# T4 taken plainly in the second group, its quarter sums spread over the third, weighings in idle PSUM banks, and the last product in column halves

## The chip, the cores and the metric

One core of one Trainium2 chip. The metric is the device time of one execution in microseconds (us). Before the change it is 1509.28 us, the median of 3 runs (1508.52 to 1510.85).

## The reference

```python
def reference(x, w):          # x: 8 x 2048 x 2048, w: 2048 x 2048, both f32
    cs = np.cumsum(x, axis=1)
    diff = cs - np.concatenate([np.zeros(...), cs[:, :-1, :]], axis=1)
    return np.matmul(diff, w).astype(np.float32)
```

The difference of a running sum is x again, so the work is one product of 16384 x 2048 by 2048 x 2048.

## The kernel before

Rows of x come in tiles of 128. Four tiles of the start are multiplied directly while w arrives. Then groups of four tiles follow: g, g+1 and h, h+1 (h = g+2). Each pair is one block product in Winograd's form, with seven half-size products where eight would be needed: B11, T1, B12 and so on are f16 blocks and sums of blocks of w, S1 to S4 sums of blocks of x. From the second group on, three of the products of each pair (with B21, B22 and T4) are split in the same way once more, which makes 28 matmuls of 2 x 16 = 32. They need the quarter sums `in2`, `in3` and `in4`, which VectorE makes once. The group that TensorE works on from about 75 to 126 us, which has none of this inner splitting yet, is called the plain group here, and the next ones the second, third and so on.

A tile of x goes through these steps: a load; a *weighing* on ScalarE (a sum of absolute values, whose elementwise output is scrap); a scale from it; a *narrowing* to f16 on ScalarE; a transpose by DMA. A weighing is either whole (`weigh`, with an output slot `c` as scrap) or in four pieces (`weigh_in`, with a pair of PSUM banks as scrap):

```python
def keep(dst, ps, scale):     # copy out of PSUM, ScalarE
    for c, p in pieces_of(dst, ps):
        after("act", lambda: nc.scalar.activation(c, p, COPY, scale=scale))

def add(dst, ps, scale):      # add out of PSUM, VectorE
    for c, p in pieces_of(dst, ps):
        after("dve", lambda: nc.vector.scalar_tensor_tensor(c, p, scale, c, MUL, ADD))

def less_in(Q1, Q2, Q4, t11, t12, t21, t22):
    less(Q1, t12, t11)        # four subtractions each
    less(Q2, t22, Q1)
    less(Q4, t21, Q2)
def less_in3(Q1, Q2, Q4, t11, t12, t21, t22):
    less(t12, t22, t12)

def weigh(t, slot):
    xf = came.pop(t)
    m, _ = after("act", lambda: measure(xf, new_c(slot)))       # one ACTIVATE of 2048
    got[t] = m, None, xf
def weigh_in(t, ps):          # cut: four ACTIVATEs of 512 into ps[i % 2], then a reduce on VectorE
    ...

def group_plain(g, X, Y, Z, V, a, b, c, d):
    # ... cut
    product(Z, S1, T1, True)
    # ... cut
    fetch_x(h + 5)
    weigh(g + 5, c)           # the first weighing that the change touches (about 116 us)
    scale_of(g + 5)
    C22 = new_c(d)
    keep(C22, Z, vh)          # TensorE's wait near 118 is for these copies
    product(X, A22g, T4, False)
    C21 = new_c(b)
    keep(C21, X, vg)
    ready(g + 5)              # the narrowing
    turn(g + 5)               # the transpose
    put(C21, g + 1, 0)
    product(Y, A21h, T3, False)
    add(C22, Y, vh)
    put(C22, h + 1, 1)
    less_in(*in2)
    less_in3(*in2)
    product(Z, S4h, B22, False)
    # ... cut
    less_in(*in3)
    product(Y, A22h, T4, False)
    # ... cut

def group(g, X, Y, Z, V, a, b, c, d):
    # ... cut
    keep(C11g, X, ug)
    S3g = sums(g, S4g)
    if second:
        weigh(h + 1, c)       # the second one (about 132 us)
        ready(h + 1)
        less_in(*in4)
    turn(h + 1)
    fetch_x(h + 4)
    product(Y, A11h, B11, True)
    if second:
        weigh_in(g + 4, V)
    # ... cut
    inner_product(A2, in2, banks, C11g, C11h, *u, between_2)
    if second:
        less_in3(*in3)
        less_in3(*in4)
    # ... cut, then four(): A22 T4 in quarters, or in the last group:
    def four_last():
        # ... cut
        product_in(q, s2, Q2, False)
        add(C21g[:, NB:], q, vg)
        put(C21g, g + 1, 0)
        product_in(Y[0], a22, Q4, False)
        keep(C21h[:, :NB], Y[0], vh)
        product_in(q, s3, Q3, False)
        for n in range(2):
            at = ds(n * NB, NB)
            add(C21h[:, at], q, vh)
            nc.scalar.dma_start(out2[ds((h + 1) * P, P), at], C21h[:, at])
```

The order of the source is not quite the order of the matmuls: the compiler moves some of TensorE's matmuls ahead of one that would wait.

Of the kernel before, what the change touches and what calls it, by code (L numbers as in the profile page):

```python
# [33 lines left out]
def kernel(  # L34
# [6 lines left out]
    nc = tc.nc  # L41
    P = 128
# [7 lines left out]
    NB = 512  # L50
# [14 lines left out]
    PLAIN = 4  # L65
# [78 lines left out]
    with tc.tile_pool(name="ring", bufs=7) as ring, tc.tile_pool(  # L144
# [97 lines left out]
        def put(c, rows, columns, queue=nc.gpsimd):  # L242
            return queue.dma_start(out2[rows, columns], c)
# [221 lines left out]
    def product(ps, a, b, first):  # L465
        for k in range(KH):
            for n in range(NH // NB):
                nc.tensor.matmul(  # L468
                    ps[n],
                    a[k],  # L470
                    b[k][:, n, :],
                    start=(first and k == 0),
                    stop=(k == KH - 1),
                    skip_group_check=True,
                )

    def product_in(ps, a, b, first):
        for k in range(4):
            nc.tensor.matmul(  # L479
                ps, a[k], b[k], start=(first and k == 0), stop=(k == 3), skip_group_check=True  # L480
            )
# [13 lines left out]
    def keep(dst, ps, scale):  # L495
        for c, p in pieces_of(dst, ps):
            after("act", lambda: nc.scalar.activation(c, p, COPY, scale=scale))  # L497

    def add(dst, ps, scale):
        for c, p in pieces_of(dst, ps):  # L500
            after(
                "dve", lambda: nc.vector.scalar_tensor_tensor(c, p, scale, c, MUL, ADD)  # L502
            )
# [9 lines left out]
    def less(dst, p, q):  # L513
        for k in range(len(dst)):
            after("dve", lambda: nc.vector.tensor_tensor(dst[k], p[k], q[k], SUB))  # L515


    def less_in(Q1, Q2, Q4, t11, t12, t21, t22):
        less(Q1, t12, t11)
# [6 lines that stand above are left out]
    def new_c(slot):  # L526
        return cpool.tile([P, NH], f32, name=f"c{slot}")
# [5 lines left out]
    def fetch_x(t):  # L533
        if t < END:
            came[t], _ = after("sp", lambda: bring(t))

    def weigh(t, slot):
        if t < END:
            xf = came.pop(t)
            m, _ = after("act", lambda: measure(xf, new_c(slot)))  # L540
            got[t] = m, None, xf
# [94 lines left out]
    def sums(t0, S4=None):  # L636
        A11, A12 = parts(t0)
        A21, A22 = parts(t0 + 1)
        total(S1, A21, A22, ADD)
        total(S2, S1, A11, SUB)  # L640
        total(A21, A11, A21, SUB)
        if S4:
            total(S4, A12, S2, SUB)
        return A21


    def group_plain(g, X, Y, Z, V, a, b, c, d):
# [67 lines left out]
        ready(h + 4)  # L715
        turn(h + 4)
        fetch_x(h + 5)
        weigh(g + 5, c)
        scale_of(g + 5)
        C22 = new_c(d)  # L720
        keep(C22, Z, vh)
# [20 lines left out]

    def group(g, X, Y, Z, V, a, b, c, d):
        h = g + 2
        second = g == PLAIN + 4
        A11g, A12g = parts(g)
        A11h, A12h = parts(h)
        A21g, A22g = parts(g + 1)
# [7 lines left out]
        C11g = new_c(a)  # L756
        keep(C11g, X, ug)
        S3g = sums(g, S4g)
        if second:
            weigh(h + 1, c)  # L760
            ready(h + 1)
            less_in(*in4)
        turn(h + 1)
        fetch_x(h + 4)
        product(Y, A11h, B11, True)
# [20 lines left out]
        total(A21h, A11h, A21h, SUB)  # L786
        total(S2, S1, A11h, SUB)
        S3h = A21h
        product(X, S3g, T3, False)
        add(C22, X, vg)  # L790
        put(C22, g + 1, 1)
# [13 lines left out]
        inner_product(A2, in2, banks, C11g, C11h, *u, between_2)  # L805
        if second:
            less_in3(*in3)
            less_in3(*in4)
        total(S4h, A12h, S2, SUB)
        turn(h + 4)  # L810
        put(C11h, h, 0)
# [1 line left out]
        one, two, A3 = sums_in(S4g, S4h, S0, S3g)  # L813
        one()
        two()

        product(Y, S2, T2, False)
        C12h = new_c(d)
# [2 lines left out]
        C22 = new_c(a)  # L821
        keep(C22, Z, vh)
        add(C12h, Z, uh)
        weigh(g + 5, b)
        one, two, A4 = sums_in(A22g, A22h, S1, S2)

# [8 lines left out]
        def seven():  # L835
            product(Y, S3h, T3, False)
            add(C22, Y, vh)
            put(C22, h + 1, 1)


        def four():
# [30 lines left out]
        def four_last():  # L872
            a11, a12, a22, s1, s2, s3, s4 = A4
            Q1, Q2, Q4, t11, Q3, t21, t22 = in4
            C21g, C21h = new_c(b), new_c(c)
            product_in(q, a11, t11, True)
            keep(C21g[:, :NB], q, vg)
            product_in(X[0], a12, t21, False)
            add(C21g[:, :NB], X[0], vg)
            product_in(X[1], s4, t22, False)  # L880
            keep(C21g[:, NB:], X[1], vg)
            product_in(e, s1, Q1, True)
            add(C21g[:, NB:], e, vg)
            keep(C21h[:, NB:], Y[1], vh)
            add(C21h[:, NB:], e, vh)
            product_in(q, s2, Q2, False)
            add(C21g[:, NB:], q, vg)
            put(C21g, g + 1, 0)
            product_in(Y[0], a22, Q4, False)
            keep(C21h[:, :NB], Y[0], vh)  # L890
            product_in(q, s3, Q3, False)
            for n in range(2):
                at = ds(n * NB, NB)
                add(C21h[:, at], q, vh)
                nc.scalar.dma_start(out2[ds((h + 1) * P, P), at], C21h[:, at])

        inner_product(A3, in3, banks, C12g, C12h, *u, between_3)
        put(C12h, h, 1)
        one()
        two()  # L900
        seven()
        (four if g + 4 < END else four_last)()

    fetch_x(PLAIN + 4)
    banks = [bank(i) for i in range(8)]
# [36 lines left out]
```

## Time and profile before

| | before |
|---|---|
| median time | 1509.28 us |
| span of the profiled execution | 1507.3 us |
| TensorE busy | 99% |
| VectorE, ScalarE busy | 73%, 57% |
| matmul to matmul, 512 columns | 0.216 us |
| one steady group, 212 matmuls | 45.80 us |

A line of the timeline gives start, duration, engine, source line, operation, output and inputs, shape and count; in brackets the idle time of the engine just before and what ended it. TensorE's ends are modelled (0.38 us for a matmul of which one starts every 0.216 us), so the bracket is some 0.16 us smaller than the true loss. Below, "wait" with three digits is the time from start to start beyond 0.216 us, and a bracket is called a bracket. The lines that the argument rests on stand in the prediction.

### The profile page before, as it was taken

The page shows a single profiled execution, that of the slowest core. Times are in us where ns is not written, and L with a number is a line of the kernel's source. Part 1 is how long each engine was busy: PE and PEld are TensorE (multiplying, and loading weights), DVE is VectorE, ACT ScalarE, POOL GpSimd, SP SyncE. Part 2 cuts the span into 40 slices and gives each one's busy share as a digit, 9 for nine tenths or more (in the row PEclk, how much of TensorE's full clock was granted, in tenths as well). Part 3 has the DMA queues.
Part 4 walks back from the last instruction along what each step waited for, and adds up shares of the span by engine and source line. Part 5 has one row for each costly group of instructions (what it writes and reads, how often), then busy time and mean ns, then how long its engine had stood idle before and what let it go on. Part 6 is the DMA issues. An engine that isn't in the chain of part 4 may idle for free.

```text
span 1507.3 us, 19123 instructions
## 1 busy us (share of the span) xinstructions
PE 1490.6 (99%) x6911; PEld 673.8 (45%) x6911; DVE 1104.4 (73%) x2053; ACT 864.5 (57%) x1107; POOL 5.2 (0%) x12
## 2 busy tenths in 40 slices
PE   8999999999999999999999999999999999999998
PEld 3444444444444444444444444444444444444443
DVE  7997777776677676777676776766776767776767
ACT  5875655565655566555656555655555565556551
POOL 0100000000000000000000000000000000000000
PEclk9999999999999999999999999999999999999999
DMA  9988878878978987888789788878788888887772
GB/s 362 351 250 233 236 224 246 234 213 227 235 225 244 224 224 236 215 246 236 210 229 232 230 241 217 235 222 248 216 244 207 236 221 250 232 236 216 223 208 112
DMA packets 322479, 351.50 MB, mean 233 GB/s; under 512 B 266896, under 2 KB 266896, under 8 KB 306512
## 3 DMA queue, kind: packets, MB, share of 16 engines
q1 hardware_dynamic: 321536, 347.92, 81.1%
q0 software_dynamic: 560, 1.84, 0.3%
q8 instruction: 54, 0.88, 0.2%
q10 hardware_dynamic: 288, 0.52, 0.1%
q14 instruction: 41, 0.34, 0.1%
HBM read 150.99 MB, written 134.22 MB: 189 GB/s over the span
## 4 chain that ended last, share of the span: by engine, by line
PE 88%; DVE 1%; DMA 1%; issue 0%; ACT 0%; DVEq 0%; ACTq 0%; SPq 0%
PE b L468 52%; PE b L479 36%; DVE c L502 1%; DMA fin<-in_x_dram 0%; DMA xT<-fin 0%; DVE W L511 0%; ACT b L553 0%; DVE W L515 0%; ACT c L497 0%; DVEq L937 0%; DVE xT L511 0%; DVE s L112 0%; DVE m L111 0%; DVE u L586 0%; DVE m L561 0%
## 5 line engine op out<-in xcount | busy, mean ns | idle before, releaser
L502 DVE SCALAR_TENSOR_TENSOR c<-b,u,c 128x512 f32<-128x512 f32 (+1 forms) x883 | 675.0, 799 | 234.8 <-ACT c L497 112.8
L497 ACT ACTIVATE c<-b,u 128x512 f32<-128x512 f32 x496 | 314.5, 680 | 265.4 <-PE b L468 170.5
L468 PE MATMUL b<-W,xT 128*128 128x512 f16 x2048 | 462.1, 379 | 0.8 <-ACT c L497 0.8
L468 PE MATMUL b<-W,W 128*128 128x512 f16 x1764 | 411.7, 379 | 1.8 <-ACT c L497 1.5
L105 ACT ACTIVATE c<-fin 128x2048 f16<-128x2048 f32 x92 | 175.7, 1910 | 242.4 <-DMA out_dram<-c 220.5
L468 PEld LDWEIGHTS <-xT 128*128 128x128 f16 x2048 | 200.4, 98 | 242.6 <-issue 1.1
L468 PEld LDWEIGHTS <-W 128*128 128x128 f16 x2016 | 197.2, 98 | 240.2 <-issue 2.1
L116 ACT ACTIVATE fin<-fin,s 128x2048 f16<-128x2048 f32 x123 | 246.3, 2002 | 93.8 <-issue 50.8
L479 PEld LDWEIGHTS <-W 128*128 128x128 f16 x1560 | 152.1, 98 | 187.5 <-issue 2.5
L479 PE MATMUL b<-W,W 128*128 128x512 f16 x810 | 220.0, 379 | 1.0 <-DVE c L502 1.0
L479 PE MATMUL b<-W,xT 128*128 128x512 f16 x720 | 180.0, 379 | 0.0
L479 PE MATMUL b<-inner,W 128*128 128x512 f16 x660 | 176.2, 379 | 0.0
L479 PEld LDWEIGHTS <-xT 128*128 128x128 f16 x960 | 93.9, 98 | 113.3
L561 DVE TENSOR_REDUCE m<-m 128x1 f32<-128x4 f32 x29 | 4.6, 157 | 106.7 <-ACT b L553 106.7
L553 ACT ACTIVATE b<-fin 128x512 f32<-128x512 f32 x116 | 67.8, 585 | 14.5 <-DMA fin<-in_x_dram 14.5
L468 PE MATMUL b<-W 128*128 128x512 f16 x252 | 75.0, 379 | 0.0
L511 DVE TENSOR_TENSOR W<-W,xT 128x1024 f16<-128x1024 f16 x122 | 68.2, 559 | 3.2
L511 DVE TENSOR_TENSOR W<-xT,W 128x1024 f16<-128x1024 f16 x122 | 67.5, 553 | 0.0
L479 PE MATMUL b<-inner,xT 128*128 128x512 f16 x240 | 61.6, 379 | 0.0
L233 PE MATMUL b<-wb,xP 128*128 128x512 bf16 x240 | 55.4, 383 | 5.9 <-ACT wb L216 4.8
L511 DVE TENSOR_TENSOR W<-xT,xT 128x1024 f16<-128x1024 f16 (+1 forms) x92 | 54.8, 596 | 0.0
L111 DVE TENSOR_SCALAR m<-m 128x1 f32<-128x1 f32 x124 | 18.5, 149 | 34.6 <-ACT c L105 33.5
(54 smaller groups left out, 457.9 us busy)
## 6 DMA issues: line engine op xcount, KB each, us to landing
out_dram<-c SPq DMA_DIRECT2D x247, 512.0 KB, 3.1
fin<-in_x_dram SPq DMA_DIRECT2D x123, 1024.0 KB, 5.5
W<-in_w_dram SPq DMA_DIRECT2D x32, 512.0 KB, 9.6
W<-in_x_dram SPq DMA_DIRECT2D x16, 256.0 KB, 7.4
xT<-fin SPq DMA_TRANSPOSE x184, 5.2
out_dram<-o POOLq DMA_DIRECT2D x7, 256.0 KB, 3.9
out_dram<-o SPq DMA_DIRECT2D x7, 256.0 KB, 4.1
xP<-in_x_dram SPq DMA_DIRECT2D x1, 1024.0 KB, 5.1
```

The lines of the kernel that those rows point to most:

```text
L105: return m, nc.scalar.activation(waste.bitcast(f16), xf, ABS, scale=1.0 / ROW, accum_out=m)
L111: nc.vector.tensor_scalar(m, m, TINY, None, MAX)
L116: return xh, nc.scalar.activation(xh, xf, COPY, scale=s)
L233: lambda: nc.tensor.matmul(ps[r][n], xP[:, r, ko, :], wb[h, ko][:, ds(n * NB, NB)], start=(ko == 0), stop=(ko == KO - 1),),
L468: nc.tensor.matmul(ps[n], a[k], b[k][:, n, :], start=(first and k == 0), stop=(k == KH - 1), skip_group_check=True,)
L479: nc.tensor.matmul(ps, a[k], b[k], start=(first and k == 0), stop=(k == 3), skip_group_check=True)
L497: after("act", lambda: nc.scalar.activation(c, p, COPY, scale=scale))
L502: "dve", lambda: nc.vector.scalar_tensor_tensor(c, p, scale, c, MUL, ADD)
L511: after("dve", lambda: nc.vector.tensor_tensor(dst.all, p.all, q.all, op))
L553: lambda: nc.scalar.activation(ps[i % 2], xf[:, at], ABS, scale=1.0 / ROW, accum_out=m4[:, i : i + 1],),
L561: after("dve", lambda: nc.vector.tensor_reduce(m, m4, AX.X, ADD))
```

## The change

It has four parts: two weighings of the warm-up move from output slots to PSUM; the second group takes A22 T4 plainly, so that T4's quarter sums are not needed until the third group; these sums are spread over the third group; and the last product runs in another order and in column halves, so that the last transfer is 128 KB in place of 256 KB.

```diff
@@ group_plain
-        weigh(g + 5, c)
+        weigh_in(g + 5, V)
@@ group
+        second, third = g == PLAIN + 4, g == PLAIN + 8
         S3g = sums(g, S4g)
+        if third:
+            less(in4[0], in4[4], in4[3])
         if second:
-            weigh(h + 1, c)
+            weigh_in(h + 1, V)
             ready(h + 1)
-            less_in(*in4)
@@ ... after total(S2, S1, A11h, SUB)
+        if third:
+            less(in4[1], in4[6], in4[0])
@@ ... after inner_product(A2, ...)
             less_in3(*in3)
-            less_in3(*in4)
@@ ... after the sums of A3
+        if third:
+            less(in4[2], in4[5], in4[1])
@@ ... before weigh(g + 5, b)
+        if third:
+            less_in3(*in4)
@@ new
+        def four_plain():
+            product(X, A22g, T4, False)
+            C21g, C21h = new_c(b), new_c(c)
+            keep(C21g, X, vg)
+            ...
+            product(Y, A22h, T4, False)
+            weigh(h + 5, d)
+            keep(C21h, Y, vh)
+            product(X, parts(g + 4)[0], B11, True)
+            ...
@@ four_last
+            product_in(q, s2, Q2, False)
+            keep(C21g[:, NB:], q, vg)
+            product_in(e, s1, Q1, True)
+            one, two = (ds(n * NB // 2, NB // 2) for n in range(2))
+            ... (copies and additions reordered) ...
             product_in(q, s3, Q3, False)
-            for n in range(2):
-                at = ds(n * NB, NB)
-                add(C21h[:, at], q, vh)
-                nc.scalar.dma_start(out2[ds((h + 1) * P, P), at], C21h[:, at])
+            keep(C21h[:, one], q[:, one], vh)
+            add(C21h[:, NB:], q, vh)
+            add(C21h[:, two], q[:, two], vh)
+            out_of(C21h, h + 1, ds(NB, NB), nc.scalar)
+            for at, ps, queue in (one, Y[0], nc.sync), (two, X[0], nc.scalar):
+                product_in(ps[:, at], a22, [b[:, at] for b in Q4], ps is X[0])
+                add(C21h[:, at], ps[:, at], vh)
+                out_of(C21h, h + 1, at, queue)
```

More of the change, by code (lines that the diff above doesn't have):

```diff
@@ L744, in group @@
         h = g + 2
-        second = g == PLAIN + 4
+        second, third = g == PLAIN + 4, g == PLAIN + 8
         A11g, A12g = parts(g)
@@ L838, in seven @@
             put(C22, h + 1, 1)
+        def four_plain():
+            product(X, A22g, T4, False)
+            C21g, C21h = new_c(b), new_c(c)
+            keep(C21g, X, vg)
+            turn(g + 5)
+            fetch_x(g + 8)
+            put(C21g, g + 1, 0)
+            product(Y, A22h, T4, False)
+            weigh(h + 5, d)
+            keep(C21h, Y, vh)
+            product(X, parts(g + 4)[0], B11, True)
+            scale_of(h + 5)
+            for t in g + 4, h + 4:
+                units[t] = unit(t)
+            put(C21h, h + 1, 0)
+            ready(h + 5)
         def four():
@@ L875, in four_last, with out_of @@
             C21g, C21h = new_c(b), new_c(c)
+            def out_of(c, t, at, queue):
+                queue.dma_start(out2[ds(t * P, P), at], c[:, at])
             product_in(q, a11, t11, True)
@@ L879, in four_last @@
             add(C21g[:, :NB], X[0], vg)
+            out_of(C21g, g + 1, ds(0, NB), nc.sync)
+            product_in(q, s2, Q2, False)
+            keep(C21g[:, NB:], q, vg)
+            product_in(e, s1, Q1, True)
+            one, two = (ds(n * NB // 2, NB // 2) for n in range(2))
+            keep(C21h[:, two], Y[0][:, two], vh)
+            keep(C21h[:, NB:], Y[1], vh)
             product_in(X[1], s4, t22, False)
-            keep(C21g[:, NB:], X[1], vg)
-            product_in(e, s1, Q1, True)
             add(C21g[:, NB:], e, vg)
-            keep(C21h[:, NB:], Y[1], vh)
             add(C21h[:, NB:], e, vh)
-            product_in(q, s2, Q2, False)
-            add(C21g[:, NB:], q, vg)
-            put(C21g, g + 1, 0)
-            product_in(Y[0], a22, Q4, False)
-            keep(C21h[:, :NB], Y[0], vh)
-            product_in(q, s3, Q3, False)
-            for n in range(2):
-                at = ds(n * NB, NB)
-                add(C21h[:, at], q, vh)
-                nc.scalar.dma_start(out2[ds((h + 1) * P, P), at], C21h[:, at])
+            add(C21g[:, NB:], X[1], vg)
+            out_of(C21g, g + 1, ds(NB, NB), nc.sync)
+            product_in(q, s3, Q3, False)
+            keep(C21h[:, one], q[:, one], vh)
[6 more added lines that the diff above has]
+                out_of(C21h, h + 1, at, queue)
         inner_product(A3, in3, banks, C12g, C12h, *u, between_3)
         put(C12h, h, 1)
-        one()
-        two()
-        seven()
-        (four if g + 4 < END else four_last)()
+        if second:
+            seven()
+            four_plain()
+        else:
+            one()
+            two()
+            seven()
+            (four if g + 4 < END else four_last)()
     fetch_x(PLAIN + 4)
```

## The prediction

> **What bounds the kernel now.** I read the page first, then TensorE's own waits, then the chain of waits, and only then the timeline around each wait that the change could touch.
>
> ```profile
> span 1507.3 us, 19123 instructions
> PE 1490.6 (99%) x6911; PEld 673.8 (45%) x6911; DVE 1104.4 (73%) x2053; ACT 864.5 (57%) x1107; POOL 5.2 (0%) x12
> ...
> PE b L233 <- ACT wb L216: 4.8, 9, 1.0
> PE b L468 <- ACT c L497: 2.3, 3, 1.3
> ...
> PE b L479 <- DVE c L502: 1.0, 3, 0.5
> ...
> 222.28 13.81 PE b L468 x64
> ```
>
> TensorE is the bound. In steady state 64 matmuls take 13.81 us, 0.216 us each, and a group of four row tiles (212 matmuls) takes 45.80 us again and again: from 222.28 to 268.08 in the chain. VectorE and ScalarE have a quarter and two fifths of the span free. After the start (the 4.8 us on ScalarE's casts, which the change does not touch) TensorE waits only about 3.3 us that the page names: 2.3 on ScalarE's copies out of PSUM and 1.0 on VectorE's additions. That is all a reordering can win, and matmuls that are added cost in full. So this is a change of tenths of a per cent.
>
> The waits lie in four places. The first is the end of the plain group:
>
> ```profile
> 115.76 1.91 ACT L105 ACTIVATE c<-fin 128x2048 f16<-128x2048 f32 x1 [1.94 <-DMA fin<-in_x_dram]
> ...
> 117.67 2.40 ACT L497 ACTIVATE c<-b,u 128x512 f32<-128x512 f32 x4
> ...
> 118.39 0.38 PE L468 MATMUL b<-W,W 128*128 128x512 f16 x1 [1.32 <-ACT c L497]
> ...
> 118.97 1.24 PE L468 MATMUL b<-W,W 128*128 128x512 f16 x5 [0.20 <-ACT c L497]
> ```
>
> ScalarE waits for a row tile of x to land (its load was issued at 109.23), weighs it for 1.91 us, and only then copies out the bank that TensorE wants. The wait was for the load, not for the output slot that serves as scrap.
>
> The second is the start of the second group, the third its second inner product:
>
> ```profile
> 131.93 1.91 ACT L105 ACTIVATE c<-fin 128x2048 f16<-128x2048 f32 x1
> ...
> 136.31 0.58 ACT L553 ACTIVATE b<-fin 128x512 f32<-128x512 f32 x1
> ...
> 138.76 3.54 ACT L497 ACTIVATE c<-b,u 128x512 f32<-128x512 f32 x6
> ...
> 140.63 3.61 PE L468 MATMUL b<-W,xT 128*128 128x512 f16 x16 [0.78 <-ACT c L497]
> ...
> 153.36 2.76 DVE L515 TENSOR_TENSOR W<-W,W 128x512 f16<-128x512 f16 x8
> ...
> 159.03 1.02 PE L479 MATMUL b<-W,W 128*128 128x512 f16 x4 [0.20 <-DVE c L502]
> ```
>
> At 140.63 TensorE waits for ScalarE, which has done a whole weighing, a narrowing (2.00) and a weighing in pieces before the copies. At 159.03 it waits for VectorE, late because of eight subtractions (2.76 us).
>
> The fourth is the end:
>
> ```profile
> 1500.94 0.69 ACT L497 ACTIVATE c<-b,u 128x512 f32<-128x512 f32 x1 [1.32 <-PE b L479]
> 1501.40 0.38 PE L479 MATMUL b<-W,W 128*128 128x512 f16 x1 [0.50 <-DVE c L502]
> ...
> 1502.53 1.41 DVE L502 SCALAR_TENSOR_TENSOR c<-b,u,c 128x512 f32<-128x512 f32 x2 [1.18 <-PE b L479]
> 1503.32 1.00 ACTq L895 DMA_DIRECT2D out_dram<-c  x2
> ```
>
> The last four matmuls wait for an addition that frees their bank; then two additions and two transfers of 256 KB end the program.
>
> **What the Trainium skill says.** "TensorE: Matmul & The Clock Gate", section "Wait — 56ns, not 53.3ns?", gives N/2.4 GHz plus about 2.5 ns from matmul to matmul, 215.7 ns at 512 columns: the trace's 216 ns agrees, so by that page a 256-column matmul should cost 109 ns (estimate; no row here has one). "ScalarE: Activation LUTs", section "What ACT_TABLE_LOAD costs", gives an ACTIVATE a fixed part of some 190 to 280 ns beside 0.833 ns an element, so four quarters cost more than one whole: the trace agrees (below). "PSUM — Partial Sum Buffer", section "PSUM bank collisions raise a hardware error", says that two engines must not touch a bank at the same time, readers included; in the trace VectorE's addition at 203.81 starts only when ScalarE's copy of the same bank, begun at 203.09, is over.
>
> **The change part by part.**
>
> *Weighings in PSUM.* Two whole weighings become four pieces each. Whole: 115.76 to the next ScalarE instruction at 117.67, 1.91 us. In pieces: 136.31 to 138.76, 2.45 us. So each lengthens ScalarE's row by 0.54 us. The scrap slot that it avoids was not waited for in either place (1.94 us for x; no gap at 131.93). At 115.76 TensorE has nothing else it may do (its other banks wait too), so the wait at 118.39 grows: **+0.54 us**. At 131.93 there is also a reduction on VectorE before the scale (0.16 us and a gap of 0.03), so the copies come 0.73 us later. There the compiler can fill: bank pair V is free, and it already pulled one matmul of the inner product ahead (at 139.47). Three more matmuls, 0.65 us, fit: **+0.1 us** (0 to 0.73).
>
> *T4 plainly in the second group.* Seven quarter products of 4 matmuls (28) become two products of 16 (32): four more at 0.216, **+0.86 us**. With them go the subtractions for T4 in the second group (12 of them at 134.24 to 138.3, where VectorE was not what TensorE waited for, and 4 of the 8 at 153.36). Those 4 take 1.38 us off VectorE before 158.23, more than the 0.36 us by which the matmul at 159.03 came late (the gap of 0.20 beyond the modelled end of the one before): **-0.36 us**. In the third group the same place costs 0.02 us.
>
> *Sums in the third group.* Sixteen subtractions at 0.336 us from start to start, 5.4 us, in four portions. Two fall where VectorE idles: after the first sums (idle 180.33 to 184.09) and after the inner sums (2.65 us idle before 203.81): free. The other two fall in rows without a gap: between the sum that ends at 190.72 and the additions that now begin at 190.63 (they overlap by a pipeline's length), and after the first two additions from 203.81. Each delays the additions that free bank q by 1.34 us, and in steady state the matmul that wants q has no slack (it starts 0.05 us after the addition ends). But the matmuls of the trace are not in the source's order: from 203.97 three matmuls of a later product stand ahead of a blocked one, and they fill its wait nearly exactly. The compiler fills such waits where it foresees them, and here it has a free bank's product and the next outer product to pull forward. **+0.1 us** (0 to 1.4).
>
> *The last product in column halves.* The column count is the same: 24 matmuls at 0.216 and 8 at 0.109 are 6.05 us, as 28 at 0.216 are. The wait at 1501.40 (0.67 us from start to start beyond one matmul) goes, since copies on ScalarE free the bank earlier. But the additions behind it queue up. From the start of the last product (1495.56) the third quarter's bank q is full after 5.4 us; ScalarE's copy of 256 columns takes an estimated 0.47 us (0.68 for 512 at 0.86 ns a column less), VectorE's addition of 512 columns 0.66, then three of 256 columns at an estimated 0.39 apart (0.66 less 256 at 1.04 ns), the last with 0.09 of tail: 5.95 + 0.66 + 3 x 0.39 + 0.09 = 7.87 us, against 8.39 (1503.94) before. With a last transfer of 128 instead of 256 KB, some 0.2 us sooner, that is **-0.7 us**.
>
> Sum: 0.54 + 0.1 + 0.86 - 0.36 + 0.1 - 0.7 = +0.5 us. On the median of 1509.28 that is **1509.8 us**.
>
> **The rivals.** *The weighings were held by output slots after all.* For it: the name of the change, and 220.5 us of ScalarE idle on transfers of c in the whole program; the slot of 131.93 had its transfer end only about half a microsecond earlier. Against it: neither of these two places shows the wait. If it held, the waits at 118 and 140 would go (1.84 and 0.95 us from start to start beyond one matmul), and the time would be 1509.28 - 2.79 + 0.86 - 0.36 + 0.1 - 0.7 = 1506.4. *Nothing is filled in the third group.* For it: no slack at q in steady state. Against it: the pulled-ahead matmuls. Then +2.7 us more, 1512. *The end is hidden by the store's latency.* A transfer of 256 KB lands about 2.4 us after issue, so halving it may win nothing; then the end gives 0.5 and the time is 1510.0.
>
> **Range and chances.** The before runs spread over 2.3 us, and one stall of 0.5 us at 651 is a transfer's chance. The parts' spreads (0.7, 1.4, 0.4) and the first rival give 1507.0 to 1511.8 for 8 in 10. A change of 2% would be 30 us, ten times every wait in reach: within 2% 0.99, faster 0.004, slower 0.006.
>
> **What would show it right or wrong.** Right: TensorE's wait on the copies at about 118 grows to some 1.9 us; ScalarE shows four pieces there after the same wait for x; the wait near 159 is gone; the second group is four matmuls longer; the third is at most 0.3 us over 45.80 and its matmuls are in another order; the last addition ends about 7.9 us after the last product began. Wrong: ScalarE weighing without the wait for x at 115; a wait for VectorE of over 1 us at q in the third group; additions at the end that do not queue; a stall in any later group.

## The result, and the profile after

The changed kernel takes 1511.15 us in the median of three runs (1511.15, 1510.03, 1511.31). The ratio of the two, computed as the mean time of one kernel's fast runs over that of the other's of the same rounds (so not quite the ratio of the medians), is 1.0008, with a 95% interval of 0.9986 to 1.0031: the same. The profiled execution has a span of 1509.4 us, 2.1 more than before. In five later executions it was 1510.21 in the median (below, after_again).

TensorE's waits on the other engines, from the waits view of the changed kernel (total, times, longest):

```profile
PE b L468 <- ACT c L497: 1.8, 2, 1.6
...
PE b L479 <- DVE c L502: 0.4, 1, 0.4
```

Before, these two stood at 2.3 and 1.0. So the named waits became shorter and the kernel did not. The timeline says where the time went, place by place. First the end of the plain group, changed kernel:

```profile
115.96 0.60 ACT L553 ACTIVATE b<-fin 128x512 f32<-128x512 f32 x1 [1.71 <-DMA fin<-in_x_dram]
...
118.42 2.39 ACT L497 ACTIVATE c<-b,u 128x512 f32<-128x512 f32 x4
...
119.14 0.38 PE L468 MATMUL b<-W,W 128*128 128x512 f16 x1 [1.64 <-ACT c L497]
...
119.71 1.58 PE L468 MATMUL b<-W,W 128*128 128x512 f16 x5 [0.20 <-ACT c L497]
```

ScalarE waits for the load of x as before, then weighs in pieces for 2.46 us (115.96 to 118.42) where the whole weighing took 1.91, and TensorE's wait grows from 1.84 to 2.16 us. This was predicted. What follows it was not. Engine busy time in the stretch from 120 to 124 us, first after, then before (the last three columns are the mean granted TensorE clock, the DMA share and GB/s):

```profile
120.00:124.00 4.00, 4.00 (x13) 1.45 (x12) 4.00 (x12) 2.70 (x3) 0.00 (x0) 0.57 0.81 267
```

```profile
120.00:124.00 4.00, 4.00 (x20) 1.83 (x19) 4.00 (x13) 1.96 (x2) 0.00 (x0) 1.00 0.95 294
```

TensorE counts as busy all the time in both, but does 13 matmuls where it did 20, at a clock of 0.57. The matmuls from 120.66 to 123.99 stand 0.427 us apart. From the second matmul after the wait to the start of the next stretch of W products there are 13.59 us before (118.97 to 132.56) and 15.28 after (119.71 to 134.99): 1.69 us lost to the clock.

Part of it did not cost anything. Before, TensorE waited 0.945 us near 140 and 0.13 near 147. In this execution it comes to 140 so late that neither wait is left, and it passes from one group into the next without a gap:

```profile
138.88 3.19 PE L468 MATMUL b<-W,W 128*128 128x512 f16 x14
...
140.25 2.39 ACT L497 ACTIVATE c<-b,u 128x512 f32<-128x512 f32 x4
...
141.90 0.38 PE L479 MATMUL b<-W,xT 128*128 128x512 f16 x1
```

Near 159 VectorE has four subtractions less (1.42 us at 155.30 for four in place of 2.76 for eight), and TensorE's bracket there is gone:

```profile
158.74 0.38 PE L479 MATMUL b<-W 128*128 128x512 f16 x1
158.95 0.38 PE L479 MATMUL b<-W,W 128*128 128x512 f16 x1
```

In the third group the waits are 0.075, 0.068 and 0.112 us. In the fourth, which the prediction thought untouched, there are 0.17 us at 234.94 and 0.53 at 241.29. They come down a chain of ScalarE and the DMA queue, of which these are lines, after and then before:

```profile
198.38 1.91 ACT L105 ACTIVATE c<-fin 128x2048 f16<-128x2048 f32 x1 [6.70 <-DMA out_dram<-c]
...
218.63 3.85 SPq L127 DMA_TRANSPOSE xT<-fin  x2
...
224.64 0.34 SPq L99 DMA_DIRECT2D fin<-in_x_dram  x1
...
231.18 0.60 ACT L553 ACTIVATE b<-fin 128x512 f32<-128x512 f32 x1 [2.28 <-DMA fin<-in_x_dram]
...
241.29 0.59 PE L479 MATMUL b<-W,W 128*128 128x512 f16 x2 [0.37 <-DVE c L502]
```

```profile
195.13 1.91 ACT L105 ACTIVATE c<-fin 128x2048 f16<-128x2048 f32 x1 [5.32 <-DMA out_dram<-c]
...
215.45 2.96 SPq L127 DMA_TRANSPOSE xT<-fin  x2
...
221.65 0.34 SPq L99 DMA_DIRECT2D fin<-in_x_dram  x1
...
228.27 0.60 ACT L553 ACTIVATE b<-fin 128x512 f32<-128x512 f32 x1 [1.45 <-DMA fin<-in_x_dram]
```

The subtractions of the third group stand ahead of additions whose results are stored; the store of a slot ends later, so the weighing that uses the slot as scrap waits 6.70 us where it waited 5.32. Behind it the stores and transposes in the DMA queue come later, and so does the load that waits for a transpose to land: it is issued 2.99 us later than before (224.64 against 221.65), while TensorE itself runs some 2.1 us later at this place. For that load ScalarE waits 2.28 us at 231 where it waited 1.45. The copies out of PSUM come behind that weighing.

The end, changed kernel:

```profile
1502.61 3.36 DVE L502 SCALAR_TENSOR_TENSOR c<-b,u,c 128x512 f32<-128x512 f32 x6
...
1503.34 1.04 PE L479 MATMUL b<-inner,xT 128*128 128x256 f16 x8
1503.54 0.47 ACT L497 ACTIVATE c<-b,u 128x256 f32<-128x256 f32 x1 [0.96 <-PE b L479]
```

The additions queue up without a gap and end at 1505.97, 7.89 us after the last product's first matmul (1498.08); before it was 8.39. Eight matmuls of 256 columns take 8 x 0.109 us. From that first matmul to the landing of the last transfer it is 10.04 us, before 10.89: 0.85 less. But the program ends 1.26 us after that landing, where it was 0.90. The trace shows why: the ending engine checks the semaphores of the transfers one by one, 0.06 us each. Before, the last one to land was the last in its row. After, six more check instructions (of up to two semaphores each) stand behind it, 6 x 0.06 = 0.37 us.

The sum, after less before, in the two profiled executions (waits from start to start):

| place | us |
|---|---|
| the start, which the change does not touch | +0.42 |
| wait near 118 (1.84 to 2.16) | +0.32 |
| half clock, 120.66 to 123.99 | +1.69 |
| waits near 140 and 147, absorbed by it | -1.08 |
| wait near 159 (0.36 to 0.02) | -0.34 |
| four more matmuls (A22 T4 plainly) | +0.86 |
| third group | +0.24 |
| fourth group | +0.69 |
| a wait near 651 that only the profile of before has | -0.50 |
| a wait at 1111 that only this one has | +0.24 |
| the end to the last landing | -0.85 |
| semaphores behind the last landing | +0.37 |
| sum | +2.06 |

The spans differ by 2.04 us, so the sum closes.

### The profile page after: what moved, and what is told of

Same layout as the page of the kernel before. It is cut to its first block, busy times and chain, and to the rows that moved or that the text cites. A ratio compares the mean times of both kernels' runs of the same rounds, so it can differ in the third digit from the quotient of the medians.

```text
span 1509.4 us, 19143 instructions
## 1 busy us (share of the span) xinstructions
PE 1495.5 (99%) x6919; PEld 676.0 (45%) x6919; DVE 1100.1 (73%) x2048; ACT 865.6 (57%) x1120; POOL 5.0 (0%) x12
## 3 DMA queue, kind: packets, MB, share of 16 engines
q0 software_dynamic: 560, 1.84, 0.3%
## 4 chain that ended last, share of the span: by engine, by line
PE 93%; DMA 2%; DVE 2%; ACT 2%; issue 1%; SPq 0%; DVEq 0%; ACTq 0%
PE b L468 55%; PE b L479 35%; PE b L233 3%; DMA fin<-in_x_dram 1%; DVE c L502 1%; DMA xT<-fin 1%; ACT wb L216 1%; DVE W L337 1%; DMA W<-in_w_dram 0%; DVE W L515 0%; DVE W L511 0%; ACT b L553 0%; SPq L127 0%; PE b L195 0%; ACT c L497 0%
## 5 line engine op out<-in xcount | busy, mean ns | idle before, releaser
L497 ACT ACTIVATE c<-b,u 128x512 f32<-128x512 f32 (+1 forms) x497 | 315.0, 680 | 263.6 <-PE b L468 176.3
L105 ACT ACTIVATE c<-fin 128x2048 f16<-128x2048 f32 x90 | 171.9, 1910 | 237.3 <-DMA out_dram<-c 217.6
L553 ACT ACTIVATE b<-fin 128x512 f32<-128x512 f32 x124 | 72.7, 586 | 15.4 <-DMA fin<-in_x_dram 14.7
L511 DVE TENSOR_TENSOR W<-W,xT 128x512 f16<-128x512 f16 (+1 forms) x121 | 67.7, 560 | 3.2
L511 DVE TENSOR_TENSOR W<-xT,W 128x512 f16<-128x512 f16 (+1 forms) x121 | 67.0, 554 | 0.0
L479 PE MATMUL b<-inner,xT 128*128 128x512 f16 (+1 forms) x240 | 60.6, 375 | 0.0
L511 DVE TENSOR_TENSOR xT<-xT,xT 128x1024 f16<-128x1024 f16 x62 | 42.6, 688 | 1.0
```

What stands on the lines that cost most here:

```text
L105: return m, nc.scalar.activation(waste.bitcast(f16), xf, ABS, scale=1.0 / ROW, accum_out=m)
L479: nc.tensor.matmul(ps, a[k], b[k], start=(first and k == 0), stop=(k == 3), skip_group_check=True)
L511: after("dve", lambda: nc.vector.tensor_tensor(dst.all, p.all, q.all, op))
L553: lambda: nc.scalar.activation(ps[i % 2], xf[:, at], ABS, scale=1.0 / ROW, accum_out=m4[:, i : i + 1],),
```

## The experiments

Theories. Mine, from the prediction: the first weighing in pieces costs since it stands ahead of the copies; the wait near 140 belongs to the weighings and not to the subtractions; the 159 wait belongs to the subtractions; the end gives its part. The rivals: the weighings were held by output slots; the subtractions share in the wait near 140; and, new after the profile, the half clock is either a consequence of the wait near 118 or an accident of this execution. "vs before" below is the mean of a kernel's five runs less the mean of the nine runs of the kernel before in the same rounds on the same chip. The runs of e1 to e4 shared one chip, those of e5 to e8 a second, after_again, e9 and e10 a third; e11 ran on a fourth. All results were correct. The 95% intervals reach some 1.9 us to either side, so of all the differences against before only those of e8 and e11 exclude zero; what the other runs show is in their timelines.

### e1_t4_only: only the T4 part

```diff
 # the changed kernel, with
-        weigh_in(g + 5, V)
+        weigh(g + 5, c)
-            weigh_in(h + 1, V)
+            weigh(h + 1, c)
 # and with four_last() of the kernel before
```

> The kernel before with T4 plainly in the second group and the subtractions spread over the third, both weighings whole and the old end. My theory (each part acts where it lies, and the waits at about 118 and 140 belong to the weighings): the wait near 118 stays at 1.8 us from start to start, no stretch of half clock after it, the wait near 140 stays at 0.9 us because VectorE's twelve subtractions had no part in it, the wait near 159 goes (-0.36), four matmuls more (+0.86), up to 0.3 us in the third group and some 0.6 us of waits in the fourth, because delayed additions in the third make a store, a weighing and a load late: together +1.2 to +1.5 us over before. Rival (the subtractions of the second group held its start): the wait near 140 falls below 0.3 us and the sum is +0.3 to +0.6. Second rival (the fourth group's waits were chance): fourth group without wait, +0.6.

Measured: 1510.08 us in the median, vs before +0.69, ratio 1.0004 (0.9991 to 1.0016), where +1.2 to +1.5 was expected. The timeline of e1:

```profile
140.72 3.61 PE L468 MATMUL b<-W,xT 128*128 128x512 f16 x16 [0.90 <-ACT c L497]
```

```profile
239.89 0.59 PE L479 MATMUL b<-W,W 128*128 128x512 f16 x2 [0.37 <-DVE c L502]
```

The wait near 140 is 1.06 us without any subtraction for T4 before it (0.945 with them), so the subtractions had no part in it. The wait near 159 is gone, the third group shows the same 0.07, 0.07 and 0.11, and the fourth group the same 0.53: these belong to the T4 part. 0.86 - 0.36 + 0.25 + 0.53 makes 1.28, of which only 0.69 show in the time. The wait of 0.5 near 651 is missing in this profile too, which would make up the rest.

### e2_weighings_only: only the two weighings

```diff
 # the kernel before, with
-        weigh(g + 5, c)
+        weigh_in(g + 5, V)
-            weigh(h + 1, c)
+            weigh_in(h + 1, V)
```

> The kernel before with only the two weighings in pieces in PSUM. My theory: the wait near 118 grows by 0.3 to 0.5 us to 2.1 to 2.4 us from start to start; after it the granted clock is about half for some 3 us in most executions (it was in the changed kernel's profile, clock 0.57 from 120 to 124, and not in before's); four matmuls instead of one are pulled ahead near 140. With the half clock the wait near 140 is gone, because TensorE is late itself, and the time is +1 to +1.5 us; without it the wait near 140 is about 1.0 us and the time +0.5 us. Rival (the weighings were held by output slots and the half clock was chance): no half clock in any execution, wait near 118 not above 1.9 us, time 0 to -1 us.

Measured: 1510.16, vs before +0.99, ratio 1.0006 (0.9993 to 1.0020). The wait near 118 grew to 2.39 us from start to start (2.03 of it here, the rest one matmul later), the wait near 140 was 0.985:

```profile
119.28 0.38 PE L468 MATMUL b<-W,W 128*128 128x512 f16 x1 [1.87 <-ACT c L497]
```

The rival of the output slots would have removed both, and is dead. But the profile shows the full clock from 120 to 124, against my expectation, and the time is above the +0.5 us that I expected for a full clock. One of the five runs (1511.47) had a mean clock of 0.998; the others 0.999 to 1.000. The half clock thus does not come in each execution.

### e3_end_only: only the new end

```diff
 # the kernel before, with four_last() of the changed kernel
```

> The kernel before with only the new end. My theory: nothing changes before the last product; from its first matmul to the landing of the last transfer 10.0 us instead of 10.9, but 0.4 us of it is lost again because the engine that ends the program checks six more semaphores after the one that lands last: -0.5 us in the span. Rival (the store's latency hides it): from the first matmul to the landing 10.6 us or more, 0 to -0.2 us in the span.

Measured: 1508.72, vs before -0.54, ratio 0.9996 (0.9983 to 1.0008). As expected: 0.85 won before the last landing, 0.37 lost behind it. The wait inside the last product is 0.08 us in place of 0.67. The profiled execution was the slowest of the five (1510.12), with waits of 0.5 us at 652 and 1339 and a longer one near 140 (1.53) that none of its code explains.

### e4_first_whole: the changed kernel with its first weighing whole again

```diff
-        weigh_in(g + 5, V)
+        weigh(g + 5, c)
```

> The changed kernel with only its first weighing (plain group) whole again. My theory: wait near 118 back to 1.8 us, no half clock in any execution, wait near 140 up to 1.0 us (TensorE is no longer late there, and four matmuls fill what one filled): -0.5 to -0.9 us against the changed kernel's slow executions, about the time of its one execution with full clock (1510.0). Rival (the half clock is chance, not the longer wait): half clock appears here as often as in the changed kernel, and the time does not differ from it by more than 0.3 us.

Measured: 1509.55, vs before +0.18, ratio 1.0000 (0.9988 to 1.0013). The wait near 118 is 1.75 us, the clock full, the wait near 140 0.98. Undoing this one line brings the changed kernel back to the time of before, as far as the intervals can tell; the wait in the fourth group is 0.29 us here, where it was 0.53; the part that takes a slot's place in PSUM was the wrong one to choose at this spot, since nothing waited for the slot.

### e5_sums_in_gaps: T4's sums where VectorE is idle

```diff
 # e4, with the four portions of the third group taken out, and
@@ group, four_plain
             product(X, parts(g + 4)[0], B11, True)
+            less_in(*in4)
@@ group, after S3g = sums(g, S4g)
         if third:
-            less(in4[0], in4[4], in4[3])
+            less_in3(*in4)
```

> The last kernel (changed, first weighing whole), with T4's twelve subtractions in the second group's plain T4 products, where VectorE has nothing to do, and the last four in the third group's first gap. My theory (the subtractions before additions make a store, a weighing and a load late, and the fourth group pays): no wait over 0.1 us in the third group and none at about 240 in the fourth, -0.5 to -0.8 us against the last kernel, 1508.9. Rival (those waits were chance of transfers): the wait of 0.3 to 0.5 us near 240 is still there, less than 0.3 us gained.

Measured: 1509.24, vs before -0.14, ratio 0.9999 (0.9987 to 1.0012). The waits of the third and the fourth group are all gone, so both came from where the sums stood. The profile has the wait near 652 again (0.53), so of the 0.54 us removed by name about 0.3 shows in the time.

### e6_copies_first: the copies ahead of the first weighing

```diff
 # e5, with, in group_plain
-        weigh(g + 5, c)
-        scale_of(g + 5)
-        C22 = new_c(d)
+        C22 = new_c(c)
         keep(C22, Z, vh)
         ...
         keep(C21, X, vg)
-        ready(g + 5)
-        turn(g + 5)
-        put(C21, g + 1, 0)
+        weigh_in(g + 5, V)
         product(Y, A21h, T3, False)
         add(C22, Y, vh)
+        put(C21, g + 1, 0)
         put(C22, h + 1, 1)
+        scale_of(g + 5)
+        ready(g + 5)
+        turn(g + 5)
 # slots c and d exchanged
```

> e5 with ScalarE's two copies out of PSUM ahead of the plain group's weighing, the output slots of the two last results exchanged so that the first copy does not wait for a store that lands at 117.1, and the weighing in PSUM. My theory (TensorE's wait near 118 is only the order on ScalarE, copies behind a weighing whose x lands at 115.7): no wait near 118 (-1.75 us), but the wait near 140 grows from 1.0 to about 1.5 us, since ScalarE and VectorE get there only 1.2 us earlier: -1.1 to -1.4 us against e5, 1507.7. Rival (the load or the store sets the pace, not the order): a wait of over 0.7 us stays near 118 or the store's landing moves it a little later; less than 0.6 us gained.

Measured: 1508.85, vs before -0.12, ratio 0.9999 (0.9987 to 1.0012): nothing against e5, where 1.1 to 1.4 us were expected. The wait near 118 is gone, and another stands 14 us later:

```profile
132.64 0.60 PE L468 MATMUL b<-W,W 128*128 128x512 f16 x2 [1.77 <-DVE W L511]
```

TensorE now waits for VectorE's sums of a tile of x (1.93 us), then 0.76 near 141 and 0.24 near 159. The wait was not removed, it turned into another. Two causes were open: VectorE being busy with `in3`'s sums, or the tile coming late. The trace of e6 has both: the transposed tile landed at 129.83, and VectorE, at work without a gap since 118.58, came to it at 131.18. So in e6 the row of sums was what ended last.

### e7_in3_later: VectorE's sums for B22 out of the way

```diff
 # e6, with
@@ group_plain
-        less_in(*in3)
@@ group, if second:
             ready(h + 1)
+            less_in(*in3)
```

> e6 with the twelve subtractions for B22's quarters moved from the end of the plain group to the place in the second group that T4's left. My theory (the start of the second group waits for VectorE's row of subtractions, through a scale that ScalarE's first copy needs, and then for ScalarE's weighing and narrowing): ScalarE's first copy of the second group starts as soon as TensorE's product is there, the waits near 140 and 147 are below 0.3 us: -1.2 to -1.6 us against e6, 1506.3, the fastest so far. Rival (ScalarE's own row of weighing, narrowing, weighing is too long whatever comes before): the wait near 140 stays above 0.8 us, less than 0.7 us gained.

Measured: 1509.96, vs before +0.69, ratio 1.0005 (0.9992 to 1.0017). A miss: with VectorE's row out of the way, the tile is what comes late. The timeline of e7:

```profile
122.92 6.07 SPq L127 DMA_TRANSPOSE xT<-fin  x2
...
131.00 0.69 DVE L511 TENSOR_TENSOR W<-xT,xT 128x1024 f16<-128x1024 f16 x1 [3.23 <-DMA xT<-fin]
...
137.29 0.60 ACT L553 ACTIVATE b<-fin 128x512 f32<-128x512 f32 x1 [1.18 <-DMA fin<-in_x_dram]
```

VectorE is idle for 3.23 us and waits for the transposed tile, which lands at 130.97; in e5 it landed at 126.64, though its issue began only 0.83 us sooner (122.09). In e6 and e7 I had put two stores of 512 KB ahead of the transpose in the queue. They landed at 127.9 and 129.1, the transpose behind them. The load of the next tile came behind the transpose, and TensorE waited 2.59 us near 141 (0.76 in e6) for copies that stand behind the weighing of that tile.

### e8_weigh_twice: the suspected wait made longer on purpose

```diff
 # the changed kernel; the first weighing's four pieces are done twice (the result stayed correct)
-            for i in range(4):
+            for i in list(range(4)) * times:
...
-        weigh_in(g + 5, V)
+        weigh_in(g + 5, V, 2)
```

> The changed kernel with the plain group's weighing done twice over (the same values). My theory of the half clock (it follows a wait of TensorE that fills a stretch of a running measurement of some 3 to 4 us, so a wait of 2.2 us gets it sometimes, a longer one always): the wait near 118 is 4.5 us, half clock follows in the profile and in every execution, the wait near 140 is gone: 1.5 to 3 us over the changed kernel. Rival (chance unrelated to the wait): clock near 1.0 from 121 to 125 in the profile, and only the 2.45 us of the second weighing lost.

Measured: 1512.81, vs before +3.67, ratio 1.0024 (1.0011 to 1.0038). Mean clocks of its five runs 0.997, 0.998, 0.999, 0.997, 0.999. The timeline and, with the columns as above, the busy time by stretches of e8:

```profile
121.00 2.72 PE L468 MATMUL b<-W,W 128*128 128x512 f16 x6 [4.17 <-ACT c L497]
```

```profile
120.00:122.00 2.00, 0.99 (x3) 0.40 (x3) 1.49 (x5) 2.00 (x6) 0.00 (x0) 0.50 0.89 348
122.00:124.00 2.00, 2.00 (x7) 0.64 (x5) 2.00 (x7) 2.00 (x3) 0.00 (x0) 0.50 0.34 143
124.00:126.40 2.40, 2.40 (x7) 0.83 (x6) 2.40 (x9) 0.56 (x1) 0.00 (x0) 0.52 0.26 53
```

A wait of 4.33 us is followed by half clock for over five, and the wait near 140 is gone again. With the changed kernel's profile this makes the half clock a consequence of TensorE's idle time. I had expected it in every execution; by the mean clocks it came in at least three of these five (two stand at 0.999, a value that runs with a full clock in their profile's stretch show too).

### after_again: the changed kernel once more

> The changed kernel once more, beside before in the same rounds. Half clock as a matter of where the wait of 2.2 us falls: the executions spread over 1.0 us or more, 1509.8 to 1511.4, whether or not this profile shows the half clock after 119; with full clock the wait near 140 is 1.0 us, with half clock below 0.3. Rival (the half clock comes every time): this profile shows it and all executions lie above 1510.7.

Measured: 1510.21 in the median (1509.84 to 1510.30), vs before +0.66, ratio 1.0004 (0.9992 to 1.0017). The stretch from 120 to 124 us:

```profile
120.00:124.00 4.00, 4.00 (x20) 1.86 (x19) 4.00 (x12) 2.79 (x3) 0.00 (x0) 1.00 0.78 264
```

The same kernel, with a wait of 2.23 us near 118, at full clock. So the half clock is a state that a wait of this length brings in some executions and not in others (the section on why the prediction was right or wrong says by what). With it out of the way the predicted order shows: four matmuls of the inner product pulled forward instead of one (140.30), and then a wait of 0.989 us where it was 0.945. The spread of 1.0 us or more that I had expected did not come: the five executions lie within 0.46 us.

### e9_narrow_first: the transpose ahead of the stores

```diff
 # e7, with, in group_plain
         keep(C22, Z, vh)
+        weigh(g + 5, b)
+        scale_of(g + 5)
+        ready(g + 5)
         product(X, A22g, T4, False)
         ...
-        weigh_in(g + 5, V)
+        turn(g + 5)
+        put(C21, g + 1, 0)
 # and without the later weighing's ready and turn
```

> e7 with the row tile that is weighed in the plain group narrowed and transposed before anything else: copy, weighing (whole), narrowing, then the second copy, and its transpose ahead of the stores on the queue. My theory of why e7 lost (the transpose of that tile was put behind two stores and landed at 131 instead of 126.5, so that VectorE's sums, and TensorE, waited for it at 132.5, and all of ScalarE's row after it came late): the transpose lands by 125.5, the wait near 132 is gone and that near 140 is below 0.5 us: -2.5 to -3.3 us against e7, 1506.8. Rival (ScalarE's row alone is too long): the wait near 132 is gone but near 140 it stays above 1 us; 1508.3.

Measured: 1507.80 in the median (one of five at 1510.31, clock 0.998), vs before -1.15, ratio 0.9992 (0.9980 to 1.0005). The transpose landed at 126.3, the wait near 132 is gone: with VectorE's row out of the way (e7), the queue's order was its cause. Waits of 1.43 and 0.36 us near 139 for the copies on ScalarE remain, as the rival said; the gain on e7, each against its own kernel before, is 1.8 us where 2.5 to 3.3 were expected.

### e10_all_in_gaps: without the plain T4 at all

```diff
 # the kernel before, with the new end, slots c and d exchanged, weigh_in(h + 1, V), and
@@ group_plain
-        weigh(g + 5, c)
-        scale_of(g + 5)
+        less_in(*in2)
+        less_in3(*in2)
         keep(C22, Z, vh)
+        weigh(g + 5, b)
+        scale_of(g + 5)
+        ready(g + 5)
 # (and both removed further down)
@@ group, if second:
             less_in(*in4)
+            less_in3(*in3)
```

> The kernel before with the new end, the copy ahead of the plain group's weighing with the slots exchanged and the narrowing first, the second weighing in PSUM (its slot's store lands at 131.5), the sums of B21's quarters in VectorE's six idle microseconds ahead of the weighing, those for B22's last quarter in the second group's first gap; T4 stays in seven quarter products everywhere. My theory (the waits were order, so that they can go without the four matmuls): no wait over 0.5 us between 90 and 1490: 1.84 + 0.95 + 0.13 + 0.36 for the waits and 0.5 for the end, -3.0 to -3.9 us against before, 1505.5. Rival (VectorE is now too full in the second group): a wait of over 0.7 us on VectorE between 130 and 170; -2 us or less.

Measured: 1507.79 (1507.51 to 1508.29), vs before -1.58, ratio 0.9989 (0.9976 to 1.0003), half of the -3.0 to -3.9 expected. The four matmuls of the plain T4 are saved again, since the sums fit into gaps of VectorE. What remains of the waits, from its timeline:

```profile
127.95 1.27 ACT L497 ACTIVATE c<-b,u 128x512 f32<-128x512 f32 x2 [2.51 <-DMA out_dram<-c]
...
139.22 0.38 PE L468 MATMUL b<-W,xT 128*128 128x512 f16 x1 [1.05 <-ACT c L497]
```

ScalarE waits for a store, then does two weighings and a narrowing ahead of the copies that TensorE wants at 139.

### e11_copies_first_twice: the same order in the second group

```diff
 # e10, with, in group
         product(Y, A11h, B11, True)
-        if second:
-            weigh_in(g + 4, V)
         C11h = new_c(b)
         ...
         keep(C12g, X, ug)
+        if second:
+            weigh_in(g + 4, V)
+            scale_of(g + 4)
```

> e10 with the same cure at its one remaining wait: in the second group ScalarE copies its two results out before it weighs the next tile, not after. My theory (this wait, too, is the order on ScalarE: the weighing waits for an x that lands at 134.8, and the copies that TensorE needs stand behind it): no wait over 0.3 us between 97 and 240, the wait of 1.2 + 0.4 us near 139 gone, -1.3 to -1.6 us against e10, 1506.3, some 3 us below before and 4 below the changed kernel. Rival (the work put off comes back: VectorE's inner sums, which wait behind the weighing's scale, are now late): a wait of over 0.7 us on VectorE between 140 and 150, less than 0.8 us gained.

Measured: 1507.22 (1506.39 to 1507.85), vs before -2.53, ratio 0.9982 (0.9969 to 0.9996). From its timeline:

```profile
146.24 0.59 PE L479 MATMUL b<-W,W 128*128 128x512 f16 x2 [0.93 <-DVE c L502]
```

The wait near 139 is gone (1.58 us in all), and 1.09 us of it come back at 146, where VectorE's additions are late behind the weighing's small operations. Against its own chip's kernel before it is 0.95 us better than e10 was against its own, where 1.3 to 1.6 were expected. It is the best version, 2.5 us below the kernel before. That is 0.2%.

## Why the prediction was right or wrong

The time was right: 1509.8 predicted, 1511.15 and 1510.21 measured in two rounds, both inside the range of 1507.0 to 1511.8, though the first came close to its upper edge for a reason that the prediction did not have. In part this is luck: the fourth group's waits, the half clock and the checks at the end were in none of its terms and only stayed within a range of 4.8 us, and neither round can tell +0.5 us from nothing (the interval of the first is -2.1 to +4.7 us).

| term | predicted | measured | shown by |
|---|---|---|---|
| first weighing in pieces | +0.54 | +0.32, +0.39, +0.55 | after, after_again, e2 |
| second weighing in pieces | +0.1 | +0.04, -0.08 | e2 and after_again against before, e4 against e1 |
| four more matmuls | +0.86 | +0.86 | all with plain T4 |
| subtractions off VectorE near 159 | -0.36 | -0.34 | after, e1 |
| sums in the third group | +0.1 | +0.24 | after, e1 |
| fourth group | 0 | +0.69, +0.60, +0.53 | after, after_again, e1; gone in e5 |
| half clock | 0 | +1.69 in some executions, net +0.6 | after, e8; not e2, after_again |
| the end | -0.7 | -0.85 + 0.37 = -0.48 | after, e3 |
| sum at full clock | +0.54 | +1.3 by waits, +0.66 by time | after_again |

*Weighings.* Right in mechanism: TensorE had nothing else to do at 118, and four pieces took 0.55 us longer. The rival of the slots was refuted by e2. The size is on or under the term and differs from profile to profile; the idle time that the load of x ended differs too (1.71 us in one, 1.95 in another), but I did not test that this is why.

*The compiler.* Right: it pulled four matmuls forward at 140 instead of one, and filled most of the additional delay; it changed the order of the third group's matmuls in the same way.

*The third group.* The step "the matmul that wants q has no slack, but is filled" held, with 0.24 us left over. The step that failed is that the matter ends with the third group. The prediction followed the additions to the bank that they free, and not to the slot that they complete: the store of the slot, the weighing into it, the narrowing, the transpose and the next load were on the same chain, and gave 0.6 us back one group later. It had itself named "a stall in any later group" as the sign of its being wrong. Moving the sums to idle stretches (e5) removed both.

*The end.* The queue of additions was right to 0.02 us (7.87 predicted, 7.89 measured), and so were the two estimates in it: the copy of 256 columns took 0.47 us, and a matmul of 256 columns 0.109 us, the figure worked out from the Trainium skill's "TensorE: Matmul & The Clock Gate", section "Wait — 56ns, not 53.3ns?". The last transfer gave more than the 0.2 us that the prediction put in without a source: it landed 2.12 us after its issue's start, where the one of 256 KB took 2.47, so that 0.35 us of the 0.85 come from it. What failed is that the program ends when the last transfer lands: 0.37 us of semaphore checks stand behind it.

*The half clock* was in no step. The same page says in its section "What's actually happening" that an idle window of about 3.4 us brings half clock and that the window runs freely. The trace agrees with the length and with the free running, and shows how much idle time it took here. A packed trace holds the granted clock as stretches with start, length and share. In all 14 profiles each stretch of full clock, and each of half clock before the program's end, is a whole multiple of 3.413 us long (438 times that before; 30, 1 and 406 times after), so the clock changes on a grid of 3.413 us, which lies differently in every execution. TensorE's idle time within one cell of that grid (waits from start to start, as above) sorts the cases:

| profile | cell | idle in it | clock in the next cell |
|---|---|---|---|
| after_again (its wait of 2.23 lies across a line) | 114.48 to 117.89, then to 121.31 | 0.54, then 1.69 | full |
| e3 | 117.01 to 120.43 | 1.99 | full |
| e2 (0.36 of its 2.39 fall into the next cell) | 115.86 to 119.27 | 2.02 | full |
| after | 117.06 to 120.47 | 2.16 | half |
| e8 | 116.07 to 119.48 | 2.81 | half |

From the first full clock to the end of every profile, no cell with up to 2.02 us was followed by half clock, and every one with 2.10 us or more was (but for after and e8, these are the cells at the programs' ends). So it is not the length of one wait that decided, but how much idle time fell into one cell: the two waits of after, 1.80 and 0.36 us, did what the single one of 2.03 in e2 did not. In the profile where it came, it cost 1.69 us and hid 1.08 us of waits behind it, so the net was 0.6 us. With the wait at 1111, this is the difference of 0.9 us between the spans of the changed kernel's two profiles (1509.4 and 1508.5).

Open are these points. The wait of 0.5 us near 651 is in the profiles of before, e2, e3, e5, e10 and e11 and not in those of the changed kernel, e1, e4 and e6 to e9; no code of the change is near it, and one profile of each kernel cannot say if it belongs to a kernel or to an execution. It would make up most of what lies between the +1.3 us by waits and the +0.66 us by time. And where between 2.0 and 2.1 us of idle time in a cell the half clock sets in was not measured, nor in how many of the executions without a profile it came.

## What to carry to other kernels

Where a bound engine waits for copies out of PSUM, put work that nobody waits for (here the measuring of the next tile) behind them, and look at the engine's own queue before giving it another scratch buffer: the slot had not been the wait. When a wait is removed or VectorE's work moved, follow the result further than the bank that it frees, through store, slot, weighing, transpose and load, since that chain took back the gain in e7 and in the fourth group; and keep a transpose that somebody waits for ahead of stores in its queue. An addition to a short wait of TensorE can cost more than its length if the clock falls, so waits that add up to some 2 us within 3.4 us deserve to be removed first.

## What the Trainium skill lacked or had wrong

- "TensorE: Matmul & The Clock Gate" (section "What's actually happening") gives one idle window of about 3.4 us, running freely, for the fall to half clock. The grid of 3.413 us agrees; what the section does not say is how idle such a window has to be. Here 2.16 us of idle time in it were enough (3.4 us at a pitch of 0.427 us for a matmul followed), and 1.99 and 2.02 us were not.
- "ScalarE: Activation LUTs" says that an ACTIVATE can have an accumulator output, but not what it costs. Here each ACTIVATE with one is followed by a read of the accumulator of 0.19 us, which starts 0.06 us before the ACTIVATE ends, and 0.09 us before whose end the next one starts; four pieces of 512 columns, of 0.58 us each, so start 0.61 us apart.
- No page that I found tells how a program's end checks its transfers: one check instruction after the other, 0.06 us each, so that a last landing early in that row costs what stands behind it, here 0.37 us.
